# Output projection to gate and up: the decode rows of h stored from another queue, the first pair's gate and up alternating per operand, memory and pools rearranged

## The chip, the core and the metric

The kernel runs on one core of a Trainium2 chip. The metric is device time in microseconds (us), the median over runs of the whole kernel. The core's engines are TensorE (PE in the rows; its weight loads are PEld), VectorE (DVE), ScalarE (ACT), GpSimd (POOL) and SyncE (SP). Each works through its own instructions in a fixed order. Transfers (DMA) are started by an engine and then run by themselves; those that SyncE starts are one queue (SPq), those that GpSimd starts another (POOLq).

## The reference

One step of a hybrid decoder, for 2048 prompt tokens and 8 decode tokens, width 1024 and feed-forward width 2816:

```python
n = rmsnorm(x)
u = n @ w_in                       # one projection, split among A and B
A = sliding-window softmax attention (window 128, sinks, relative bias)
B = gated linear attention (chunked recurrence)
h = x + concat(A, B) @ w_o
z = rmsnorm(h)
y = h + (silu(z @ w_gate) * (z @ w_up)) @ w_down
```

The outputs are y for prompt and decode tokens, and the new key, value and state caches. All of it is float32.

## The kernel before, in words

**Numbers.** A float32 product is made of three matmuls in a faster type. Each operand is split in a high and a low part: ScalarE casts (L92), VectorE subtracts (L93); `mm3` issues high by high, high by low, low by high (L104 to L106).

**Stages.** Projection and attention come first, then gated linear attention, whose results `mix_d` lie in memory off the core. Then come the three stages near the change.

*Output projection* (the block that begins at L963). The tokens are 16 tiles of 128, taken in the order 0, 4, 1, 5, 2, 6, 3, 7, 8, 12 and so on to 11, 15, and then the eight decode rows (tile `NB`). `load_tile` loads a tile of `mix_d` (L995), splits it to `mt` and loads x into `h` (L1000). `product` (L1009) multiplies with the output weights `WO0` and `WO1`, adds into `h` and stores h for the last stage (L1022; for the decode rows to `hdec_d`). `normalise` (L1025) squares on ScalarE, takes the reciprocal root, scales to `z` (L1032), transposes by TensorE (`ps_zT`, L1037) and copies into the blocks `b0` to `b3`. `operands` (L1045) makes seven operands from the four blocks of a tile pair, splits each into a buffer `zhl` and stores it from GpSimd into `zc_d` (L1057). `zhl` comes from a pool of three buffers, so that the fourth operand is cast when the first one's store has landed. The decode rows' four columns per block are appended to the operands of the last tile pair, (1, 3) in the code.

*Gate and up* (the block that begins at L1166). The product z times the weights is done in a Strassen form: seven products P1, P6, P2, P7, P5, P4, P3 in this order (`PRODS`), each on one operand of z (`z0` to `z6`, numbered in that order) and one sum of weight blocks. Each product has its accumulator in one of three kinds of banks in PSUM: a (P1, then P2 on top of it), b (P6, P7, P4), c (P5, then P3). `ready` says what follows each: behind P1, ScalarE copies the bank to `p1` (L1149) before P2 adds into the bank; behind the others come adds on VectorE, and products of gate and up at the end. The 22 column blocks of the weights are 11 pairs (`fp`); the tokens are two halves (`sb`), the first of 512 columns in one piece, the second of 516 in two. For each half, seven loads bring `z0` to `z6` (L1242) from SyncE. For each pair, `load_w` loads four raw pieces of weights (L1179, two of gate and two of up), and `units` and `sums_a` form the sums on VectorE (`sx`, `sy`, L958 and L961) and split them to `whl`. There are four raw buffers and seven `whl` buffers.

*Down* (from L1270) loads `md_d`, forms the Strassen sums of the down weights, and adds h from memory by accumulating transfers; the decode rows go to `hdec_d` in the same manner.

**What sets the order.** The code gives the dependencies and a first order. The framework's scheduler, with a simulation of the engines, then sets the order on each engine; the program waits by semaphores. The pools lie on the right and left side of the on-core memory; where a pool of a later stage lies on the bytes of an earlier one, its first user waits for the earlier users.

**The numbers of the tiles** (as in `z4_10179`) are running numbers of the program and differ between the two kernels.

Of the kernel before, what the change touches and what calls it, by code (L numbers as in the profile page):

```python
# [51 lines left out]
def hymba_kernel(ctx: ExitStack, tc: tile.TileContext, I, O, X=None, phases=3):  # L52
# [49 lines left out]
    def mm3(ps, lh, ll, rh, rl, start, stop, more=False):  # L102

        nc.tensor.matmul(ps, lh, rh, start=start, stop=False, skip_group_check=more)  # L104
        nc.tensor.matmul(ps, lh, rl, start=False, stop=False, skip_group_check=more)  # L105
        nc.tensor.matmul(ps, ll, rh, start=False, stop=stop, skip_group_check=more)  # L106

# [856 lines left out]
    with ExitStack() as ph:  # L964


        mixp = pool(ph, "m_mix", 2, side="right")
        wop = pool(ph, "m_wo", 1, side="right")
        hlp = pool(ph, "m_hl", 3, side="right")
        hp = pool(ph, "m_h", 3, side="right")  # L970
        zp = pool(ph, "m_z", 2, side="right")
        bp = pool(ph, "m_b", 1, side="right")
        tp = pool(ph, "m_t", 1, side="right")
# [3 lines left out]

        WO = [wop.tile([P, 2, KD, 512], F32R, name=f"WO{dh}") for dh in range(2)]
        gBf = zp.tile([P, D], F32, name="gBf", bufs=1)
# [4 lines left out]
        def load_tile(ti):  # L984
            h = hp.tile([P, D], F32, tag="h", name="h")
            if ti == NB:
                nc.sync.dma_start(h[:ND], I["x_sample"].rearrange("n o d -> (n o) d"))
                return None, h

            if ti in tiles[:2]:  # L990
                mr = hlp.tile([P, 1056], F32, tag="hl", name="mr")[:, :1024]
            else:
                mr = craw.tile([P, 1024], F32, tag="raw", name="mr")
            mr = mr.rearrange("p (k t) -> p k t", k=KD)
            nc.sync.dma_start(mr, mix_d[ti])  # L995

            mt = mixp.tile([P, 2 * KD * P + 64], F32R, tag="mix", name="mt")[:, :2 * KD * P]
            mt = mt.rearrange("p (s k t) -> p s k t", s=2, k=KD)
            split(mt[:, 0], mt[:, 1], mr)
            nc.sync.dma_start(h, I["x_prompt"][0, ti * P:(ti + 1) * P, :])  # L1000
            return mt, h
# [8 lines left out]
        def product(ti, mt, h):  # L1010
            n = P if ti < NB else ND
            for dh in range(2):
# [8 lines left out]
                add_h(h, n, dh, ps)  # L1021
            nc.sync.dma_start(h_d[ti] if ti < NB else hdec_d, h[:n])  # L1022
            return h
# [142 lines left out]
    with ExitStack() as ph:  # L1166
        zcp = pool(ph, "g_zc", 1, side="right")

# [14 lines left out]

        def pair(sb, fp, zc):
            W, pieces = WIDTHS[sb], PIECES[sb]
# [17 lines left out]
            def prod(st, q, hl):  # L1203
                z = zc[q]
                hv = hl.rearrange("p s (k n) -> p s k n", k=4)
                for i, (c0, c1) in enumerate(pieces):
                    ps = st.bank(q, i)[:, :c1 - c0]
                    for k in range(4):
                        mm3(ps, hv[:, 0, k], hv[:, 1, k], z[:, 0, k, c0:c1], z[:, 1, k, c0:c1],
                            q in ("P1", "P6", "P5") and k == 0, k == 3, q not in ("P1", "P6", "P5"))  # L1210
# [27 lines left out]
        for sb in range(2):  # L1238
            zc = {name: zcp.tile([P, 2, 4, 516], F32R, tag=f"z{q}", name=f"z{q}")[:, :, :, :WIDTHS[sb]]
                  for q, name in reversed(list(enumerate(PRODS)))}  # L1240
            for q, name in enumerate(PRODS):
                nc.sync.dma_start(zc[name].bitcast(F32), zc_d[sb][q])  # L1242
            for fp in range(NP):
                pair(sb, fp, zc)

# [152 lines left out]
```

## Time and profile before

| what | value |
|---|---|
| three runs | 2311.71, 2314.23, 2313.62 us; median 2313.62 |
| the profiled execution: time, span | 2311.51 us, 2309.7 us |
| transferred in all | 364.57 MB, mean 158 GB/s |
| SyncE's queue (with the other hardware queues) | 258.80 MB, 34.2% of 16 DMA engines |
| GpSimd's queue | 103.55 MB, 17.9% |

The span is the time from the first to the last recorded instruction; 1.8 us of the execution lie outside it. In this span the output projection's last prompt tile ends at 938 us, pair 0 of gate and up begins at 959, and the down stage's first loads come about 1850. In rows of waits, the three numbers behind the colon are the sum of the idle time in us, the number of waits and the longest. In rows of the timeline stand the start in us, the duration, the engine, the line, the operation, out<-in with shapes, the count, and in brackets the idle time ahead with what ended it. A row that begins with A:B is a stretch in us.

### The profile page before, as it was taken

The numbers are of one execution on the slowest core, as the hardware profiler recorded it, in microseconds if no ns is written. First come the engines' busy times: TensorE is split into PE (matmuls) and PEld (weight loads), VectorE is DVE, ScalarE is ACT, GpSimd is POOL, SyncE is SP. The second block draws the span as 40 slices with busy tenths as digits, with TensorE's granted clock in tenths as the row PEclk, the third lists the DMA queues.
The fourth block names the chain that finished last, engine by engine and source line by source line (L and its number), as shares of the span: only waits on it lengthen the run. The fifth ranks groups of instructions, "written<-read, shape, count | busy, mean of one in ns | idle before, by whom it ended". The sixth has DMA issues, their size and how long they took to land.

```text
span 2309.7 us, 34809 instructions
## 1 busy us (share of the span) xinstructions
PE 2227.1 (96%) x12649; PEld 1923.6 (83%) x12649; DVE 1600.5 (69%) x3236; ACT 957.2 (41%) x2120; POOL 623.8 (27%) x791
## 2 busy tenths in 40 slices
PE   8999998999999999699999999999999989999998
PEld 6888886788887788578888889999999968787887
DVE  6787887587776567556666666767676674847477
ACT  5676777343443234323232333333333243535342
POOL 2443434365465133201111110101010122222222
PEclk9999998999998999899999999999999999999999
DMA  7323234245325689872324257323233277878877
GB/s 239 122 75 115 93 108 153 90 157 165 126 87 214 225 275 288 276 247 87 119 79 127 78 177 290 110 84 115 87 111 97 83 225 171 210 165 213 185 184 263
DMA packets 204935, 364.57 MB, mean 158 GB/s; under 512 B 15411, under 2 KB 128332, under 8 KB 200780
## 3 DMA queue, kind: packets, MB, share of 16 engines
q1 hardware_dynamic: 167740, 258.80, 34.2%
q0 software_dynamic: 37024, 103.55, 17.9%
q8 instruction: 100, 1.64, 0.3%
q14 instruction: 71, 0.58, 0.1%
HBM read 211.09 MB, written 152.27 MB: 157 GB/s over the span
## 4 chain that ended last, share of the span: by engine, by line
PE 31%; issue 20%; POOL 5%; DMA 1%; DVE 0%; POOLq 0%; ACT 0%; SPq 0%; DVEq 0%; ACTq 0%
PE ps_b L105 4%; PE ps_b L104 4%; PE ps_b L106 4%; POOL h_d L1329 4%; PE ps_c L105 3%; PE ps_c L104 3%; PE ps_c L106 3%; PE ps_a L105 3%; PE ps_a L106 3%; PE ps_a L104 3%; POOL out_y_prompt_dram L1324 1%; DMA z<-zc_d_P 1%; POOL md_d L1236 1%; DMA zc_d_P<-zhl 0%; DMA wrg<-in_w_gate_dram 0%
## 5 line engine op out<-in xcount | busy, mean ns | idle before, releaser
L104 PE MATMUL ps_b<-z,whl 128*128 128x258 f32 (+1 forms) x792 | 253.8, 321 | 3.2 <-DMA z<-zc_d_P 3.2
L105 PE MATMUL ps_b<-z,whl 128*128 128x258 f32 (+1 forms) x792 | 254.0, 321 | 0.0
L106 PE MATMUL ps_b<-z,whl 128*128 128x258 f32 (+1 forms) x792 | 252.8, 319 | 0.0
L92 ACT CAST dm<-mr 128x384 fp32r<-128x384 f32 (+1 forms) x224 | 108.0, 488 | 188.4 <-PE ps_b L106 97.6
L104 PE MATMUL ps_a<-z,whl 128*128 128x258 f32 (+1 forms) x528 | 170.9, 324 | 8.3 <-DMA z<-zc_d_P 8.3
L105 PE MATMUL ps_a<-z,whl 128*128 128x258 f32 (+1 forms) x528 | 170.7, 323 | 0.0
L106 PE MATMUL ps_a<-z,whl 128*128 128x258 f32 (+1 forms) x528 | 170.3, 323 | 0.0
L104 PE MATMUL ps_c<-z,whl 128*128 128x258 f32 (+1 forms) x528 | 168.6, 319 | 0.9 <-DMA z<-zc_d_P 0.9
L105 PE MATMUL ps_c<-z,whl 128*128 128x258 f32 (+1 forms) x528 | 169.1, 320 | 0.0
L106 PE MATMUL ps_c<-z,whl 128*128 128x258 f32 (+1 forms) x528 | 168.9, 320 | 0.0
L104 PEld LDWEIGHTS ps_b<-z,whl 128*128 128x128 f32 x792 | 149.3, 189 | 15.9 <-DMA z<-zc_d_P 3.5
L106 PEld LDWEIGHTS ps_b<-z,whl 128*128 128x128 f32 x792 | 149.2, 188 | 12.1
L105 PEld LDWEIGHTS ps_b<-z,whl 128*128 128x128 f32 x792 | 149.2, 188 | 11.9
L93 DVE TENSOR_TENSOR dm<-mr,dm 128x384 fp32r<-128x384 f32 (+1 forms) x224 | 114.9, 519 | 59.4 <-ACT dm L92 59.4
L92 ACT CAST whl<-wrg 128x512 fp32r<-128x512 f32 x132 | 81.6, 620 | 150.5 <-PE ps_b L106 81.2
L802 POOL TENSOR_TENSOR bd<-E,qTb 64x128 f32<-64x128 f32 x224 | 127.1, 567 | 60.6 <-ACT E L787 47.2
L93 DVE TENSOR_TENSOR whl<-wrg,whl 128x512 fp32r<-128x512 f32 x132 | 90.9, 688 | 42.9 <-ACT whl L92 42.7
L961 DVE TENSOR_TENSOR gu<-ps_c,gu 128x512 f32<-128x512 f32 (+1 forms) x130 | 77.9, 600 | 61.0 <-PE ps_c L106 60.3
L1236 POOL DMA_DIRECT2D md_d<-m x22 | 15.7, 713 | 373.7 <-DVE m L1199 360.3
L104 PEld LDWEIGHTS ps_a<-z,whl 128*128 128x128 f32 x528 | 100.8, 191 | 17.0 <-issue 4.4
L104 PEld LDWEIGHTS ps_c<-z,whl 128*128 128x128 f32 x528 | 99.8, 189 | 9.3 <-ACT whl L92 1.3
L105 PEld LDWEIGHTS ps_a<-z,whl 128*128 128x128 f32 x528 | 100.5, 190 | 8.2
(385 smaller groups left out, 6625.9 us busy)
## 6 DMA issues: line engine op xcount, KB each, us to landing
mr<-md_d SPq DMA_DIRECT2D x24, 1344.0 KB
zc_d_P<-zhl POOLq DMA_DIRECT2D x49, 512.0 KB, 6.1
wrg<-in_w_gate_dram SPq DMA_DIRECT2D x44, 512.0 KB
wrg<-in_w_up_dram SPq DMA_DIRECT2D x44, 512.0 KB
nT_d<-nT SPq DMA_DIRECT2D x16, 1024.0 KB
zT<-nT_d SPq DMA_DIRECT2D x8, 2048.0 KB
z<-zc_d_P SPq DMA_DIRECT2D x7, 2064.0 KB
z<-zc_d_P SPq DMA_DIRECT2D x7, 2048.0 KB
```

Of the source, the lines that this page charges most:

```text
L92: nc.scalar.copy(h, src)
L93: (eng or nc.vector).tensor_tensor(l, src, h.bitcast(F32), ALU.subtract)
L104: nc.tensor.matmul(ps, lh, rh, start=start, stop=False, skip_group_check=more)
L105: nc.tensor.matmul(ps, lh, rl, start=False, stop=False, skip_group_check=more)
L106: nc.tensor.matmul(ps, ll, rh, start=False, stop=stop, skip_group_check=more)
L802: nc.gpsimd.tensor_tensor(bv[rows, :, h], eo, qo, ALU.mult)
L961: nc.vector.tensor_tensor(out, a, b, ALU.add)
L1236: nc.gpsimd.dma_start(md_d[sb][g][:, :, q, fp - GROUPS[g][0], :], src.rearrange("p (m t) -> p m t", m=4))
L1324: nc.gpsimd.dma_start(O["y_prompt"][0, ti * P:(ti + 1) * P, cols], hq[which])
L1329: nc.gpsimd.dma_start(h_d[ti][:, cols], c, accum_op=ALU.add)
```

## The change

It has five parts.

1. The decode rows' h is stored to `hdec_d` from GpSimd and no longer from SyncE.
2. The pool of `WO0` and `WO1` becomes two pools, the pool of `zhl` lies behind that of `z`, and the mix tile is padded by 96 in place of 64 elements (17152 bytes a partition in place of 16896).
3. `z0` to `z6` get a pool each, allocated from P1 on; before, they were one pool and allocated from the back. By the program's memory map, `z0` to `z2` (P1, P6, P2) now lie on the mix tiles and `WO0`, `z3` and `z4` (P7, P5) on `WO1`, `z5` and `z6` on `h`, `z` and `zhl`. Before, `z0` lay at the far end and `z4` on `zhl` buffers.
4. The raw weights of a half's first pair are loaded ahead of the loads of z in the code, and those of each further pair behind the code of the pair before it.
5. For the first half's first pair, each of the 14 products is put behind the one before it in the order (`issue_after`), so that gate and up alternate per operand.

```diff
-            nc.sync.dma_start(h_d[ti] if ti < NB else hdec_d, h[:n])
+            (nc.sync if ti < NB else nc.gpsimd).dma_start(h_d[ti] if ti < NB else hdec_d, h[:n])
```
```diff
         mixp = pool(ph, "m_mix", 2, side="right")
-        wop = pool(ph, "m_wo", 1, side="right")
-        hlp = pool(ph, "m_hl", 3, side="right")
+        wop = [pool(ph, f"m_wo{dh}", 1, side="right") for dh in range(2)]
         hp = pool(ph, "m_h", 3, side="right")
         zp = pool(ph, "m_z", 2, side="right")
+        hlp = pool(ph, "m_hl", 3, side="right")
...
-            mt = mixp.tile([P, 2 * KD * P + 64], F32R, tag="mix", name="mt")[:, :2 * KD * P]
+            mt = mixp.tile([P, 2 * KD * P + 96], F32R, tag="mix", name="mt")[:, :2 * KD * P]
```
```diff
-        zcp = pool(ph, "g_zc", 1, side="right")
+        zcp = {name: pool(ph, f"g_z{q}", 1, side="right") for q, name in enumerate(PRODS)}
...
-            ug, uu = load_w(w_g, fp), load_w(w_u, fp)
             if len(pieces) == 1:
+                last = None
                 for q in PRODS:
-                    prod(sg, q, next(ug))
-                    prod(su, q, next(uu))
+                    for st, us in ((sg, ug), (su, uu)):
+
+                        with tc.issue_after(last) if fp == 0 and last else nullcontext():
+                            last = prod(st, q, next(us))
...
         for sb in range(2):
-            zc = {name: zcp.tile([P, 2, 4, 516], F32R, tag=f"z{q}", name=f"z{q}")[:, :, :, :WIDTHS[sb]]
-                  for q, name in reversed(list(enumerate(PRODS)))}
+            zc = {name: zcp[name].tile([P, 2, 4, 516], F32R, tag=f"z{q}", name=f"z{q}")[:, :, :, :WIDTHS[sb]]
+                  for q, name in enumerate(PRODS)}
+            raws = load_w(w_g, 0), load_w(w_u, 0)
             for q, name in enumerate(PRODS):
                 nc.sync.dma_start(zc[name].bitcast(F32), zc_d[sb][q])
             for fp in range(NP):
-                pair(sb, fp, zc)
+                pair(sb, fp, zc, *raws)
+                if fp + 1 < NP:
+                    raws = load_w(w_g, fp + 1), load_w(w_u, fp + 1)
```

`mm3` returns its last matmul, and `prod` the instruction of it. From L1022 on, a line of the kernel before has a number 1 to 6 higher in the changed one (L1022 is L1023, L1057 is L1058, L1149 is L1150, L1179 is L1181, L1242 is L1248).

**SyncE, at the end of the output projection.** What stands in its order before, from the last prompt tile's store of h on (`wrg` is a raw piece of weights, the last row the first piece of pair 1):

```order
L1022 DMA h_d15_4838<-h_9846 128x1024
L1022 DMA hdec_d_4839<-h_9962 8x1024
L1242 DMA z0_10184<-zc_d0_P1_4840 128x8x512
L1242 DMA z1_10183<-zc_d0_P6_4841 128x8x512
L1242 DMA z2_10182<-zc_d0_P2_4842 128x8x512
L1242 DMA z3_10181<-zc_d0_P7_4843 128x8x512
L1242 DMA z4_10180<-zc_d0_P5_4844 128x8x512
L1242 DMA z5_10179<-zc_d0_P4_4845 128x8x512
L1242 DMA z6_10178<-zc_d0_P3_4846 128x8x512
L1179 DMA wrg_10475<-in_w_gate_dram 128x4x256
```

And in the changed kernel, at the same place (`wrg_10490` is pair 1's second gate piece, `wrg_10492` and `wrg_10494` its two up pieces):

```order
L1248 DMA z0_10200<-zc_d0_P1_4840 128x8x512
L1023 DMA h_d15_4838<-h_9849 128x1024
L1248 DMA z1_10201<-zc_d0_P6_4841 128x8x512
L1248 DMA z2_10202<-zc_d0_P2_4842 128x8x512
L1248 DMA z3_10203<-zc_d0_P7_4843 128x8x512
L1248 DMA z4_10204<-zc_d0_P5_4844 128x8x512
L1181 DMA wrg_10490<-in_w_gate_dram 128x4x256
L1181 DMA wrg_10492<-in_w_up_dram 128x4x256
L1248 DMA z5_10205<-zc_d0_P4_4845 128x8x512
L1248 DMA z6_10206<-zc_d0_P3_4846 128x8x512
L1181 DMA wrg_10494<-in_w_up_dram 128x4x256
```

The store of `hdec_d` is gone from this queue, P1's load stands ahead of the last prompt tile's store, and two of pair 1's pieces stand between the loads of P5 and P4.

**VectorE, at the operands of the last token tile.** Before (`zhl` rows are the second half of a split of these operands, `sx` is a sum of raw pieces, `gu2` the add on P6's bank of the gate):

```order
L93 TENSOR_TENSOR zhl_10134<-b1_9843,zhl_10134 128x528
L93 TENSOR_TENSOR zhl_10138<-t2_10120,zhl_10138 128x528
L93 TENSOR_TENSOR zhl_10142<-t0_10118,zhl_10142 128x528
L93 TENSOR_TENSOR zhl_10146<-t3_10121,zhl_10146 128x528
L93 TENSOR_TENSOR zhl_10150<-b3_9845,zhl_10150 128x528
L93 TENSOR_TENSOR whl_10331<-sx_10262,whl_10331 128x512
L961 TENSOR_TENSOR sx_10262<-wrg_10203,wrg_10205 128x512
L93 TENSOR_TENSOR whl_10348<-sx_10241,whl_10348 128x512
L961 TENSOR_TENSOR gu2_10194<-ps_b_10248,gp1_10193 128x512
```

And in the changed kernel (`zhl_10137` to `zhl_10153` are the same five operands; `uu2` is the add on P6's bank of up):

```order
L93 TENSOR_TENSOR whl_10407<-wrg_10209,whl_10407 128x512
L93 TENSOR_TENSOR zhl_10137<-b1_9846,zhl_10137 128x528
L958 TENSOR_TENSOR sy_10538<-wrg_10490,sx_10537 128x512
L93 TENSOR_TENSOR zhl_10141<-t2_10123,zhl_10141 128x528
L93 TENSOR_TENSOR zhl_10145<-t0_10121,zhl_10145 128x528
L958 TENSOR_TENSOR sx_10558<-wrg_10492 128x512
L93 TENSOR_TENSOR zhl_10149<-t3_10124,zhl_10149 128x528
L93 TENSOR_TENSOR zhl_10153<-b3_9848,zhl_10153 128x528
L961 TENSOR_TENSOR gu2_10224<-ps_b_10270,gp1_10223 128x512
L961 TENSOR_TENSOR uu2_10227<-ps_b_10291,up1_10226 128x512
```

Two sums of pair 1, which read `wrg_10490` and `wrg_10492`, have moved between the splits of the operands.

On ScalarE, before and now, the casts of the last tile's operands stand ahead of the copies of P1's banks. On TensorE, P1's products of gate and up (24 matmuls) now stand ahead of the transposes of the decode rows, and pair 1's first product no longer stands between products of pair 0.

More of the change, by code (lines that the diff above doesn't have):

```diff
@@ L1 @@
 import math
-from contextlib import ExitStack
+from contextlib import ExitStack, nullcontext
 import numpy as np
@@ L105, in mm3 @@
         nc.tensor.matmul(ps, lh, rl, start=False, stop=False, skip_group_check=more)
-        nc.tensor.matmul(ps, ll, rh, start=False, stop=stop, skip_group_check=more)
+        return nc.tensor.matmul(ps, ll, rh, start=False, stop=stop, skip_group_check=more)
     def rstd(ss, n, scale, cols=1):
@@ L975, in hymba_kernel @@
         acc = pool(ph, "m_acc", 4, space=PSUM)
-        WO = [wop.tile([P, 2, KD, 512], F32R, name=f"WO{dh}") for dh in range(2)]
+        WO = [wop[dh].tile([P, 2, KD, 512], F32R, name=f"WO{dh}") for dh in range(2)]
         gBf = zp.tile([P, D], F32, name="gBf", bufs=1)
@@ L1182, in load_w, with pair @@
             return units((r0[:, :, 0:P], r1[:, :, 0:P], r0[:, :, P:], r1[:, :, P:]), sums_a)
-        def pair(sb, fp, zc):
+        def pair(sb, fp, zc, ug, uu):
             W, pieces = WIDTHS[sb], PIECES[sb]
```

5 lines of the change are left out of this document (3 added, 2 removed).

## The prediction, made before the changed kernel was run

> **What bounds the kernel now.** The page comes first: how full TensorE is.
>
> ```profile
> span 2309.7 us, 34809 instructions
> PE 2227.1 (96%) x12649; PEld 1923.6 (83%) x12649; DVE 1600.5 (69%) x3236; ACT 957.2 (41%) x2120; POOL 623.8 (27%) x791
> z<-zc_d_P SPq DMA_DIRECT2D x7, 2048.0 KB
> wrg<-in_w_gate_dram SPq DMA_DIRECT2D x44, 512.0 KB
> ```
>
> TensorE is the bound; time is only won where it stands still or runs at a lowered clock. The last two rows, from the page's DMA issues, give sizes: an operand load of the first token half has 2048 KB, a raw weight piece 512 KB. Next I read TensorE's waits from 935 to 1000 us, where the change acts.
>
> ```profile
> PE ps_a L104 <- DMA z<-zc_d_P: 8.3, 2, 4.3
> PE ps_zT L1037 <- DVE z L1032: 6.9, 1, 6.9
> PE ps_b L104 <- DMA z<-zc_d_P: 3.2, 2, 3.0
> PE ps_c L104 <- DMA z<-zc_d_P: 0.9, 1, 0.9
> ```
>
> So 12.4 us go to the operand loads and 6.9 us to the normalisation of the decode rows. The stage table (PE, PEld, DVE, ACT, POOL busy, granted clock, DMA share, GB/s) shows a lowered clock too, then a saturated DMA, then a full TensorE:
>
> ```profile
> 960.00:965.00 5.00, 5.00 (x13) 3.84 (x13) 0.00 (x0) 0.32 (x1) 0.71 (x1) 0.51 1.03 373
> 995.00:1000.00 5.00, 4.07 (x18) 3.03 (x17) 1.99 (x3) 0.62 (x1) 0.00 (x0) 1.00 1.04 397
> 1000.00:1020.00 20.00, 20.00 (x88) 16.18 (x87) 11.72 (x20) 6.92 (x12) 1.42 (x2) 1.00 0.58 198
> ```
>
> TensorE's timeline dates each landing by the matmul that waited for it: the last prompt tile's last matmul, then the first matmuls of P1, P6, P2, P7, P5, then pair 1's first and one after pair 0's last product.
>
> ```profile
> 937.38 0.39 PE L106 MATMUL ps_wo<-WO,mt 128*128 128x512 f32 x1
> 959.10 0.80 PE L104 MATMUL ps_a<-z,whl 128*128 128x512 f32 x1 [4.28 <-DMA z<-zc_d_P]
> 964.81 0.46 PE L105 MATMUL ps_a<-z,whl 128*128 128x512 f32 x1
> 970.62 0.51 PE L104 MATMUL ps_b<-z,whl 128*128 128x512 f32 x1 [3.02 <-DMA z<-zc_d_P]
> 982.03 0.76 PE L104 MATMUL ps_a<-z,whl 128*128 128x512 f32 x1 [4.03 <-DMA z<-zc_d_P]
> 989.61 0.47 PE L104 MATMUL ps_b<-z,whl 128*128 128x512 f32 x1 [0.23 <-DMA z<-zc_d_P]
> 996.34 0.47 PE L104 MATMUL ps_c<-z,whl 128*128 128x512 f32 x1 [0.93 <-DMA z<-zc_d_P]
> 1001.98 0.40 PE L104 MATMUL ps_a<-z,whl 128*128 128x512 f32 x1
> 1015.92 0.40 PE L104 MATMUL ps_a<-z,whl 128*128 128x512 f32 x1
> ```
>
> P5's 24 matmuls take 1001.98 - 996.34 = 5.64 us, 0.235 us each. From 996.34 on nothing waits. At 1015.92 pair 0 is done and 12 matmuls of pair 1 besides (2.8 us), so the mark for equal work is 1013.1: "pair 0 done, nothing more". The forecast is the difference of that mark.
>
> The reason for the late loads is SyncE's queue:
>
> ```profile
> SPq L1022 <- DVE h L582: 11.4, 1, 11.4
> ```
> ```profile
> 950.34 0.29 SPq L1022 DMA_DIRECT2D hdec_d<-h  x1
> 950.81 15.16 SPq L1242 DMA_DIRECT2D z<-zc_d_P  x4
> 991.56 5.48 SPq L1179 DMA_DIRECT2D wrg<-in_w_gate_dram  x1
> ```
>
> The decode rows' store waits 11.4 us for its add, with the seven loads behind it.
>
> **What the change takes away.** The store leaves that queue, and P1's load now waits only for the mix tiles: 937.38 + 0.39, so it is issued at 937.8 instead of 950.81, 13.0 us earlier. The store's place on GpSimd is before the decode rows' reciprocal root; its data is ready at 950.3, the root's about 1.2 us later, and an issue takes 0.85 us: nothing. TensorE's order puts P1 ahead of the decode transposes, which covers the 6.9 us. P6 and P2 need WO0 free, P7 and P5 WO1, each free by 946; P5's load no longer waits for operand stores. Taken alone these edits win what the loads come earlier.
>
> **What it adds.** The rows of order show two pieces of pair 1's raw weights between P5's and P4's loads, and on VectorE two sums of pair 1 that read them, between the operand stores of the last token tile. Both are new places. Does a piece behind P5's load land behind it? Before, the first such piece was issued at 991.56, behind all seven loads; this is its sum on VectorE:
>
> ```profile
> 1009.75 0.69 DVE L958 TENSOR_TENSOR sy<-wrg,sx 128x512 f32<-128x512 f32 x1 [1.29 <-DMA wrg<-in_w_gate_dram]
> ```
>
> It took 18.2 us, 13.4 us after P5's load: the queue delivers in turn. That gives prices: two loads and one piece (a quarter of a load) in 13.41 us are 5.96 us a load and 1.5 us a piece. Beside stores it is dearer:
>
> ```profile
> 938.03 0.85 POOL L1057 DMA_DIRECT2D zc_d_P<-zhl  x1 [0.34 <-DVE zhl L93]
> ...
> 947.30 0.85 POOL L1057 DMA_DIRECT2D zc_d_P<-zhl  x1 [1.46 <-DVE zhl L93]
> ...
> 976.67 0.85 POOL L1057 DMA_DIRECT2D zc_d_P<-zhl  x1 [3.53 <-DVE zhl L93]
> ```
> ```profile
> zc_d_P<-zhl POOLq DMA_DIRECT2D x7, 528.0 KB, 9.4
> ```
> ```profile
> DMA to landing us min/median/max: 4.2/7.5/10.8
> ```
>
> Seven stores fall beside P6's and P2's loads, which took 982.03 - 959.10 = 22.93 us: (22.93 - 11.92) / 7 = 1.57 us a store. P1's own 8.29 us are a load, a store and 0.7 us to start.
>
> Now the new wait, step by step.
> 1. P5's load lands: 937.8 + 0.7 + five loads 29.8 + the last h store 1.5 + seven stores 11.0 (four issued from 938.03 to 947.30, three of the last tile before the sum) = 980.8. The piece behind it: 982.3. It has been issued in time: it needs P6's up product, which ends near 966 (P1's load 950.8, P1 with a cold clock, P6).
> 2. VectorE stands at the sum until then. Behind it wait four operand splits of the last tile, then the adds on P6's bank. Sum and next split 2 x 0.69 = 1.4: 983.7.
> 3. The split's store takes 7.5 us to land: 991.2. There are three hl buffers, so the fourth of these operands is cast only when this store has landed.
> 4. ScalarE casts in that order and copies P1's bank behind the casts. Before, it was so too:
>
> ```profile
> 963.96 0.63 PE L106 MATMUL ps_a<-z,whl 128*128 128x512 f32 x1
> ```
> ```profile
> 974.71 0.63 ACT L92 CAST zhl<-b 128x528 fp32r<-128x528 f32 x1 [3.45 <-DMA zc_d_P<-zhl]
> 975.25 0.58 ACT L1149 COPY gp<-ps_a 128x512 f32<-128x512 f32 x1
> ```
>
> P1's gate product ended at 964.6, and its copy ran at 975.25, right behind the last cast; then it cost nothing, since P2's load came at 982.03. P2 adds into the same bank and must wait for the copy. Cast and copy 1.2: P2 starts at 992.4.
> 5. Five products of 24 matmuls: 28.2. TensorE has stood still for some 26 us and is cold: after the wait at 959.10 thirteen matmuls took 5.71 us to 964.81 instead of 3.06, so 2.6. Pair 0 ends at 1023.2, **10.1 us behind** the mark of 1013.1.
>
> On step 5, the Trainium skill, "TensorE: Matmul & The Clock Gate", "Part 1: The HAM clock gate", says that an idle window of about 3.4 us halves the clock and 3.4 us of work restore it. By that the cold start would lose 1.7 instead of 2.6 us and the sum would be 9.2, an estimate from the page; the row here shows a longer cold stretch, 5.7 us.
>
> Bounds. The loads with stores, h and piece are 15.25 MB; at the table's best 397 GB/s 38.4 us, so the piece at 976.9; a store landing in 4.2; 1.5 us for the cold start (seven slow matmuls after 982.03): +0.3 us in all. Upwards: three loads at 11.5 us as seen beside stores, then 7.6 and 6.7, the h store, the piece and 0.7: 990.2; a store in 10.8: +21.3 us. I take the middle prices, measured on the same kinds of transfer.
>
> What is late next: P4's bank also waits for a sum that reads the third piece, behind P3's load, behind the last operand store. That store 1000.0, load 1006.7, piece 1008.2, sum and add 1009.6; P4 is due at 992.4 + 2.6 + 16.9 = 1011.9. Cover 2.3 us; with a store of 10.8 us it is gone and costs 1.0.
>
> Elsewhere. At the projection's start WO1 is loaded first and tile 4's split comes earlier, which covers 1.1 us, but tile 1's mix load now stands behind tile 4's h store:
>
> ```profile
> 757.15 0.50 PE L106 MATMUL ps_wo<-WO,mt 128*128 128x512 f32 x1 [1.14 <-DVE mt L93]
> 771.82 0.50 PE L104 MATMUL ps_wo<-WO,mt 128*128 128x512 f32 x1 [3.02 <-ACT mt L92]
> ```
> ```profile
> 765.69 2.50 SPq L995 DMA_DIRECT2D mr<-mix_d  x3
> 768.68 0.32 SPq L1022 DMA_DIRECT2D h_d<-h  x1
> ```
>
> That can be 3.0 us later and lengthen the 3.02 us wait. Between -1.1 and +3.0 I take 0, since both are near. In down the decode matmuls move a few places within a stretch that stands still for its loads:
>
> ```profile
> 1850.00:1860.00 10.00, 6.48 (x16) 3.97 (x17) 10.00 (x20) 6.63 (x14) 2.32 (x4) 0.54 1.01 396
> ```
>
> I take 0, with -1 to +1. The second half's loads, the padding and the split pools in themselves cost nothing: TensorE waits for no operand load there.
>
> **The sum.** The profiled execution's own time, 2311.5 us (span 2309.7), plus 10.1 is 2321.6. The three runs' median is 2313.6, 2.1 above it; on it the forecast is 2323.7.
>
> **Rivals.**
> *The loads win* (12 in 100, faster). If the piece overtakes P5's load, because it is small or the sixteen DMA engines don't keep step, VectorE never holds ScalarE. It decides at P2's start: earlier than 982.7 wins. Then P5 starts at 980.8, P4's load (two pieces ahead) lands at 989.8, P3's at 995.8, pair 0 ends at 1001.4: 11.7 us won, 2301.9. For it speak 13 us of earlier issue; against it the piece at 1009.75, which did not overtake. The Trainium skill, "DMA: Bandwidth & Descriptors", "Two DMAs through the same engine are not ordered", says that nothing orders DMAs across the 16 engines; the trace shows no overtaking.
> *It cancels out* (16). Fast stores (4.2 us) and loads at 397 GB/s bring P2 to 984 to 987: between +0.3 and +4.6, about 2316.
> *A second wait* (8). The thin cover goes and the early stage takes its 3.0 us besides: 10.1 + 1.0 + 3.0 or more, about 2328 and beyond.
> *The forecast* has 64.
>
> **How the numbers follow.** 0.2% is 4.6 us, about what a measurement of this kernel tells from no change. Slower by more: 64 and 8 of the cases, 0.72. Within: 0.16. Faster: 0.12. The range leaves out the faster case and the far end of the bounds: 2313 to 2332.
>
> **What would show it.** A wait of TensorE at P2's first matmul of 20 us or more, put down to ScalarE's copy of P1's bank; on VectorE an idle time ended by a raw gate piece, in the middle of the last tile's splits, near 982; P1's first matmul near 951. No wait for the decode transposes. Wrong: P2 starting on its load, or the sum on VectorE finding its piece before 975.

## The result, and the profile after

The changed kernel took 2328.71 us (median of 4 runs, 2327.68 to 2331.72) against 2313.93 for the kernel before on the same chip. The ratio is 1.0073, 95% interval 1.0060 to 1.0086: **14.8 us slower**. The forecast was 10.1 us slower (2323.7, range 2313 to 2332). The profiled executions differ by more, 2329.41 - 2311.51 = 17.9 us, because before's profiled run lies 2.4 us below the median of its four runs and after's 0.7 above. One execution in the whole set, in experiment 11, took 5114.89 us and is in no ratio.

The page of the changed kernel: the same matmuls and bytes in a longer span.

```profile
span 2327.6 us, 34823 instructions
PE 2228.0 (96%) x12649; PEld 1926.0 (83%) x12649; DVE 1598.7 (69%) x3236; ACT 957.4 (41%) x2120; POOL 623.0 (27%) x792
```

TensorE's waits from 930 to 1040 us (sum, number, longest) answer to the four rows of before:

```profile
PE ps_a L104 <- ACT gp L1150: 28.0, 1, 28.0
PE ps_a L104 <- DMA z<-zc_d_P: 6.5, 1, 6.5
```

Before, 12.4 us went to operand loads and 6.9 to the decode rows. Now one wait of 28.0 us stands there, and what ends it is ScalarE's copy of P1's bank. TensorE's timeline gives the places: the last prompt matmul, P1's first matmul, the decode transposes, P2's first matmul, the first matmul behind pair 0, the last matmul of the kernel.

```profile
940.94 0.39 PE L106 MATMUL ps_wo<-WO,mt 128*128 128x512 f32 x1
...
957.02 0.77 PE L104 MATMUL ps_a<-z,whl 128*128 128x512 f32 x1 [6.52 <-DMA z<-zc_d_P]
...
965.22 0.66 PE L1038 MATMUL ps_zT<-ident,z 8*128 8x8 f32 x8
999.75 0.80 PE L104 MATMUL ps_a<-z,whl 128*128 128x512 f32 x1 [27.98 <-ACT gp L1150]
...
1029.39 0.40 PE L104 MATMUL ps_a<-z,whl 128*128 128x512 f32 x1
...
2316.30 0.39 PE L106 MATMUL ps_c<-dhl,dm 128*128 128x512 f32 x1
```

Pair 0 ends at 1029.39, 16.3 us behind the mark of 1013.1. The chain that leads to 999.75 is read backwards on ScalarE, GpSimd, VectorE and SyncE. ScalarE's last operand cast and, right behind it, the copy:

```profile
998.58 0.63 ACT L92 CAST zhl<-b 128x528 fp32r<-128x528 f32 x1 [14.39 <-DMA zc_d_P<-zhl]
999.12 0.58 ACT L1150 COPY gp<-ps_a 128x512 f32<-128x512 f32 x1
```

The cast had waited 14.4 us for a store to free a buffer. That store is the first of these three, issued by GpSimd, which had waited 16.5 us for the split:

```profile
991.39 2.68 POOL L1058 DMA_DIRECT2D zc_d_P<-zhl  x3 [16.48 <-DVE zhl L93]
```

The split stood on VectorE behind the sum of pair 1, and the sum behind its raw piece:

```profile
973.07 0.70 DVE L93 TENSOR_TENSOR zhl<-b,zhl 128x528 fp32r<-128x528 f32 x1
989.78 0.69 DVE L958 TENSOR_TENSOR sy<-wrg,sx 128x512 f32<-128x512 f32 x1 [16.01 <-DMA wrg<-in_w_gate_dram]
990.39 1.32 DVE L93 TENSOR_TENSOR zhl<-t,zhl 128x528 fp32r<-128x528 f32 x2
```

VectorE did nothing for 16.0 us, with a ready split behind the waiting sum. SyncE's queue shows why the piece came so late; it stands behind P5's load:

```profile
941.36 0.59 SPq L1248 DMA_DIRECT2D z<-zc_d_P  x1
942.09 0.58 SPq L1023 DMA_DIRECT2D h_d<-h  x1
945.94 21.99 SPq L1248 DMA_DIRECT2D z<-zc_d_P  x4
968.03 10.10 SPq L1181 DMA_DIRECT2D wrg<-in_w_gate_dram  x1
```

P1's load is issued 9.4 us earlier than before (941.36 against 950.81), yet P1 starts only 2.1 us earlier (957.02 against 959.10). The stage table (PE, PEld, DVE, ACT, POOL busy, granted clock, DMA share, GB/s) from 940 to 990, before:

```profile
940.00:990.00 50.00, 31.55 (x117) 22.56 (x115) 21.54 (x37) 15.49 (x26) 9.68 (x12) 0.80 0.97 318
```

and in the changed kernel:

```profile
940.00:990.00 50.00, 25.17 (x110) 17.46 (x108) 18.94 (x33) 11.06 (x19) 8.52 (x11) 0.79 1.02 339
```

The DMA engines were at 0.97 of their time in this stretch already (the share is a sum of the packets' times and can pass 1). They are at 1.02 now; there was hardly a gap for the earlier loads to fill.

**The account.** Every kernel here has 12649 matmuls, so the start of the same-numbered matmul can be compared with before's. The table gives what each stage adds, in us, for the profiled execution of each kernel. The stages are cut at the matmuls that start, in before's profile, at 730 (9 us ahead of the projection's first), at 790 (in the projection's fourth tile), at 920 and at 1021 (so that the block holds pair 0); then come the start of down, 1840 to 1920, and what lies between the last matmul and the end. What a table row leaves over is at most 0.7, but for 2.1 of "pad 64" at the end of down. The names are those of the experiments below.

| kernel | to 730 | to 790 | to 920 | block | down's start | last matmul, in all | behind it |
|---|---|---|---|---|---|---|---|
| after | +1.3 | +0.8 | +1.2 | +12.9 | -2.4 | +13.8 | +4.05 |
| sums held | +1.5 | +1.3 | +1.2 | +2.4 | -1.8 | +4.4 | +4.04 |
| transposes first | -2.2 | -1.3 | +1.2 | +12.2 | -1.9 | +8.0 | +4.04 |
| both | -0.3 | -1.0 | +1.2 | +3.3 | -2.0 | +1.7 | +4.04 |
| before, GpSimd store | +1.5 | -1.4 | 0.0 | +0.6 | -0.1 | +0.6 | +4.05 |
| four buffers | +3.4 | +0.7 | +1.2 | +14.5 | -2.3 | +18.0 | +4.05 |
| pieces last | -1.0 | +0.9 | +1.2 | +12.2 | -2.0 | +11.3 | +4.05 |
| before, ScalarE store | -1.9 | +2.3 | -0.1 | 0.0 | +1.5 | +2.2 | 0.00 |
| before, GpSimd store in halves | -0.4 | -0.9 | 0.0 | +0.7 | +0.9 | +0.2 | +4.05 |
| pad 64 | +3.9 | +0.8 | -0.3 | +11.8 | -2.5 | +15.8 | +4.05 |
| before, pad 96 | -0.3 | +0.2 | +1.4 | -0.8 | 0.0 | +0.8 | +0.01 |
| held, ScalarE store | +2.2 | -0.5 | +1.1 | +4.7 | -2.4 | +5.0 | +0.05 |
| before, rows of 512 | +1.4 | -1.9 | 0.0 | +1.4 | +1.6 | -3.0 | +0.01 |

The stretch to 730 is the same code, in the same order, in all of them and varies from -2.2 to +3.9, so a single profile's total is only good to some us; the stages are compared one by one. (In the last row the stage between the block and down brings another -6.2.) For the changed kernel three terms stand out besides the block: 1.2 us inside the projection, -2.4 in down, and 4.05 us behind the last matmul. That last one is seen in two rows, the last output store and the span's end. Before (whose span ends at 2309.7):

```profile
2304.67 0.54 POOL L1324 DMA_DIRECT2D out_y_prompt_dram<-hq  x1 [0.82 <-DVE hq L961]
```

After (span 2327.6):

```profile
2318.44 0.54 POOL L1332 DMA_DIRECT2D out_y_prompt_dram<-hq  x1 [0.82 <-DVE hq L961]
```

From that store to the end it is 5.1 us before and 9.1 after. In the trace's instruction records the difference is one instruction, GpSimd's closing drain: 4.316 us before, 8.357 after.

### The profile page after: what moved, and what is told of

Read it like the earlier page. It is cut to its first block, busy times and chain, and to the rows that moved or that the text cites. A ratio compares the mean times of both kernels' runs of the same rounds, so it can differ in the third digit from the quotient of the medians.

```text
span 2327.6 us, 34823 instructions
## 1 busy us (share of the span) xinstructions
PE 2228.0 (96%) x12649; PEld 1926.0 (83%) x12649; DVE 1598.7 (69%) x3236; ACT 957.4 (41%) x2120; POOL 623.0 (27%) x792
## 4 chain that ended last, share of the span: by engine, by line
PE 58%; issue 22%; POOL 8%; DVE 5%; DMA 4%; ACT 2%; SPq 0%; POOLq 0%; ACTq 0%; DVEq 0%
PE ps_b L105 5%; PE ps_b L104 4%; PE ps_b L106 4%; POOL h_d L1337 3%; PE ps_a L105 3%; PE ps_c L105 3%; PE ps_a L104 3%; PE ps_a L106 3%; PE ps_c L106 3%; PE ps_c L104 3%; PE ps_d L104 3%; PE ps_d L106 3%; PE ps_d L105 3%; PE ps_wo L104 2%; PE ps_wo L105 2%
## 5 line engine op out<-in xcount | busy, mean ns | idle before, releaser
L105 PEld LDWEIGHTS ps_b<-z,whl 128*128 128x128 f32 x792 | 148.8, 188 | 11.8
L92 ACT CAST whl<-sy 128x512 fp32r<-128x512 f32 x88 | 54.6, 620 | 130.4 <-PE ps_b L106 86.8
```

The source lines that it names most:

```text
L92: nc.scalar.copy(h, src)
```

## The experiments

**1 to 3: is it the sum of pair 1?** In the first, pair 1's sums are put on VectorE behind the add on P7's bank of up in pair 0 (`add` returns its instruction for this); the loads stay as they are.

```diff
-                add(u3, ps, p1)
+                self.mark = add(u3, ps, p1)
...
-                            last = prod(st, q, next(us))
+                            with tc.issue_after(marks[0]) if (sb, fp) == (0, 1) else nullcontext():
+                                hl = next(us)
+                            last = prod(st, q, hl)
+                marks.append(su.mark)
```

> The changed kernel, with pair 1's first sums on VectorE put behind the P7 adds of pair 0; nothing else is edited. Theory A (the sum that waits for its piece holds the operand splits, these the store, the buffer, ScalarE and P2): VectorE's wait of 16 us for the raw piece goes; the second half-operand's store goes out near 978, lands near 987, P2 starts near 988 in place of 999.75, and the time falls by about 11.5 us from 2328.7 to 2317 (2314 to 2320). Rival B (the loads set the pace, DMA engines are full from 947 to 990, and the sum only stands in the same time): at most 3 us, 2326. Rival C (TensorE's order is the cause: P1 ahead of the decode transposes makes the operands late): no gain from this edit, 2327 to 2329.

Measured: 2319.44 against 2315.59 before on that chip, 1.0019 (1.0010 to 1.0028): some 4 us of the 14.8 are left. TensorE's waits in the block:

```profile
PE ps_a L104 <- ACT gp L1150: 16.1, 1, 16.1
```

P2 starts at 989.64 instead of 999.75, and the block costs 2.4 us instead of 12.9. The sum in the middle of the splits was the cause of 10.5 us. What holds P2 now is the same copy, behind a last cast at 988.47 that waits 3.4 us for a store. Before, that cast ran at 974.71.

In the second, P1 goes behind the decode transposes, as before the change; the scheduler then puts the sum two splits later. `zt` collects the transposes; its last is the decode rows'.

```diff
-                last = None
+                last = zt[-1]
```

> The changed kernel, with TensorE's P1 of pair 0 put behind the transposes of the decode rows, as it was before. The scheduler then also sets the sum two splits later on VectorE: the fourth and fifth operand of the last tile are split ahead of it. Theory A: operands begin 5 to 6 us earlier, ScalarE is no longer held and P2 starts near 983, but the adds on P6's bank still stand behind the sum, which waits for its piece until 990: the wait moves to P7, near 993, and the time is 2316 (2313 to 2319). Rival B (loads): 2326 or more. Rival C (the transposes alone): the whole loss and more comes back, 2309 to 2312, with no wait of VectorE for the piece that anyone waits for.

Measured: 2326.56, 1.0054 (1.0040 to 1.0067); a miss by 10 us. P2 came at 984.03, 10 us earlier than in the changed kernel once the 5.6 us are taken off by which this execution came earlier into the block; and the block still cost 12.2. VectorE's rows for the sums, in this kernel:

```profile
990.25 0.69 DVE L958 TENSOR_TENSOR sy<-wrg,sx 128x512 f32<-128x512 f32 x1 [17.12 <-DMA wrg<-in_w_gate_dram]
...
1008.92 0.69 DVE L958 TENSOR_TENSOR sy<-wrg,sx 128x512 f32<-128x512 f32 x1 [12.89 <-DMA wrg<-in_w_up_dram]
```

and TensorE's for P7 and P4:

```profile
993.69 0.50 PE L104 MATMUL ps_b<-z,whl 128*128 128x512 f32 x1 [2.29 <-DVE gu L961]
...
1010.27 0.50 PE L104 MATMUL ps_b<-z,whl 128*128 128x512 f32 x1 [3.63 <-DVE gu L961]
```

The sum no longer holds the splits, but it still holds VectorE until 990; the add on P6's bank stands behind it, and P7 needs that bank. The third piece does the same to P4 at 1008.92. The wait moved from one bank to the next. The third kernel holds the sums and puts the transposes first as well.

> Both edits together: sums of pair 1 behind the P7 adds, P1 behind the decode transposes. Theory A: P2 near 982, P7 near 988, P5 on its load near 990 to 993, pair 0 done some 18 us earlier than in the changed kernel: 2310 (2307 to 2313), below the sum of neither edit alone, since both serve the same chain. Rival B (loads): 2326. Rival C: as with the transposes alone, within 1 us of that run.

Measured: 2319.59, 1.0020 (1.0010 to 1.0029), the same as with the sums held alone, where 2310 was expected. P2 starts at 986.88, with this wait:

```profile
PE ps_a L104 <- ACT gp L1152: 12.3, 1, 12.3
```

The decode transposes being late is not what keeps the held kernel from winning: moving them up left the last cast at 985.71, 11 us later than before (974.71). The stores that these casts wait for are not slower than before: those of 528 KB take 8.8 us to land here and 9.4 before (medians). But the first of the seven casts comes 6.2 us later (960.86 against 954.69), behind 512 KB stores that take 9.7 us to land instead of 4.6, and ScalarE's rows show something more behind the second:

```profile
963.09 0.63 ACT L92 CAST zhl<-t 128x528 fp32r<-128x528 f32 x1 [1.59 <-DVE t L958]
966.24 0.62 ACT L92 CAST whl<-sx 128x512 fp32r<-128x512 f32 x1 [2.52 <-PE ps_a L106]
969.02 0.62 ACT L92 CAST whl<-sx 128x512 fp32r<-128x512 f32 x1 [2.16 <-PE ps_a L106]
971.81 0.62 ACT L92 CAST whl<-sx 128x512 fp32r<-128x512 f32 x1 [2.17 <-PE ps_b L106]
972.34 0.63 ACT L92 CAST zhl<-b 128x528 fp32r<-128x528 f32 x1
```

Three casts of weight sums, each waiting for TensorE, stand between the second and the third operand. Before, the third was cast at 957.45, right behind the second at 956.91. From the first cast to the last it is 24.9 us here and 20.0 before. The changed kernel has weight casts among the operand casts too, at 969.86 and 971.81. No run moves them away, so what they cost is not shown.

**4, 7 and 8: what are the earlier loads worth?** The kernel before, with the `hdec_d` store alone moved to GpSimd:

```diff
-            nc.sync.dma_start(h_d[ti] if ti < NB else hdec_d, h[:n])
+            (nc.sync if ti < NB else nc.gpsimd).dma_start(h_d[ti] if ti < NB else hdec_d, h[:n])
```

> The kernel before, with the one edit that the decode rows' h is stored from GpSimd. Order and memory are else those of before: the seven loads stand together, no sum of pair 1 among the splits. Theory A: P1's load goes out some 12 us earlier, P1 starts near 955, P2 on ScalarE's copy or its load near 976 to 979, P5's load still waits for the last operand's store, P5 near 991: 4 to 6 us won, 2309 (2306 to 2312). Rival B (the DMA engines are the limit): under 2 us won, 2312 to 2314. Rival D (GpSimd's queue is held by the new store and the operand stores go out later): slower than before, 2315 or more.

Measured: 2319.45, 1.0019 (1.0009 to 1.0029): slower by some 4 us, where a gain was expected; a miss. SyncE issued the loads 11.2 us earlier:

```profile
939.61 52.83 SPq L1242 DMA_DIRECT2D z<-zc_d_P  x7
```

But TensorE's timeline for P1, P6, P2 and P7 reads almost as before (959.10, 970.62, 982.03, 989.61):

```profile
959.48 0.80 PE L104 MATMUL ps_a<-z,whl 128*128 128x512 f32 x1 [2.84 <-DMA z<-zc_d_P]
969.18 0.67 PE L104 MATMUL ps_b<-z,whl 128*128 128x512 f32 x1 [2.49 <-DMA z<-zc_d_P]
979.83 0.77 PE L104 MATMUL ps_a<-z,whl 128*128 128x512 f32 x1 [3.28 <-DMA z<-zc_d_P]
990.00 0.77 PE L104 MATMUL ps_b<-z,whl 128*128 128x512 f32 x1 [2.93 <-DMA z<-zc_d_P]
```

The stage table says why:

```profile
940.00:990.00 50.00, 30.05 (x115) 21.23 (x114) 22.53 (x38) 15.59 (x26) 10.96 (x14) 0.83 1.03 327
```

The DMA engines go from 0.97 to 1.03 busy and move 327 instead of 318 GB/s: over 50 us that is 0.45 MB, about a fifth of one load. What the loads take early, the stores lose: the three 512 KB stores of `zc_d` after 940 take 10.8 us to land instead of 4.6 (medians). So the block gains nothing (+0.6). The slowdown lies at the other end of the kernel; its last output store is at 2305.24 and its span ends at 2314.4, 9.1 us later, with the drain of 8.357 us.

The same store from ScalarE's queue instead (`nc.scalar` in place of `nc.gpsimd`):

> The kernel before, with the decode rows' h stored from ScalarE's queue in place of SyncE's: the loads are freed as with the store on GpSimd, and GpSimd gets no further transfer. Theory E (found in the profiles: GpSimd's last instruction, a drain, takes 4.3 us in the kernel before and 8.4 us in every kernel with the store on GpSimd): drain 4.3 us, the time 3 to 4 us under that of the kernel before with the store on GpSimd, so the same as the kernel before within 2 us (2312 to 2316). If the drain's length is chance or a matter of timing: as with the store on GpSimd, 4 us above the kernel before. The block of pair 0 itself as there: within 1 us of before, since the DMA engines are full from 940 on.

Measured: 2314.68, 1.0001 (0.9991 to 1.0010). The last output store, in this kernel, whose span ends at 2311.9:

```profile
2306.84 0.54 POOL L1324 DMA_DIRECT2D out_y_prompt_dram<-hq  x1 [0.82 <-DVE hq L961]
```

That is 5.1 us, and the drain is 4.316 again. The loads were issued at 939.58, as early as in the other, and the block cost 0.0. So the longer drain comes with the store on GpSimd's queue, and the earlier issue is worth nothing by itself. P2 started at 978.76 here, after a wait of 6.2 us for the copy of P1's bank: even in before's order the copy is the next thing behind the loads. P7 at 989.55 was again the load's.

Is the price paid per transfer? The store from GpSimd in two halves:

```diff
-            nc.sync.dma_start(h_d[ti] if ti < NB else hdec_d, h[:n])
+            if ti < NB:
+                nc.sync.dma_start(h_d[ti], h[:n])
+            else:
+                for dh in range(2):
+                    nc.gpsimd.dma_start(hdec_d[:, dh * 512:(dh + 1) * 512], h[:n, dh * 512:(dh + 1) * 512])
```

> The kernel before, with the decode rows' h stored from GpSimd in two halves, two transfers in place of one. Theory E with a price for each transfer: the drain takes 12 us. With a fixed price for the 8-row store or its place: 8.4 us. If it hangs on whether the count is even or odd: 4.3 us again. The rest as with one store.

Measured (a single run): 2315.79, drain 8.357 again. The price is not one per transfer of this store. GpSimd starts 346 transfers before, 347 with this store and 348 with its halves; whether any other further transfer would do the same was not tried.

**5 and 6: two other ways around the sum.** A fourth buffer for the splits, at the price of one of the three `h` buffers:

```diff
-        hp = pool(ph, "m_h", 3, side="right")
+        hp = pool(ph, "m_h", 2, side="right")
...
-        hlp = pool(ph, "m_hl", 3, side="right")
+        hlp = pool(ph, "m_hl", 4, side="right")
```

> The changed kernel with four buffers for the split operands in place of three, paid for by two buffers for h in place of three. The sum of pair 1 stays where it is on VectorE. Theory A, its buffer step: the last cast on ScalarE now needs the third operand's store and no longer the fourth's, which stands behind the sum; so ScalarE copies P1's bank near 985 and P2 starts near 985 in place of 999.75, while VectorE still waits for the piece until 990, and the adds on P6's bank make P7 wait until 993 or 994: 10 to 13 us of the block come back, 2316 to 2319, plus 0 to 4 us if two h buffers hold the projection up. Rival B (the loads): P2 and P7 move by under 3 us. If the buffer step is wrong, and ScalarE or P2 hangs on VectorE directly: P2 stays at 999.

Measured: 2333.51 against 2314.66, 1.0080 (1.0064 to 1.0096); a miss, slower than the changed kernel. TensorE's waits:

```profile
PE ps_b L104 <- DVE gu L961: 11.3, 2, 7.4
PE ps_a L104 <- ACT gp L1150: 11.1, 1, 11.1
```

P2 came at 987.72, 12 us earlier than in the changed kernel, though this execution came 2.0 us later into the block; so the buffer step of the chain is real. The block cost 14.5 all the same: the sums, at 996.00 and 1018.73, now held P7 and P4 by VectorE's adds.

Pair 1's pieces put behind all seven loads on SyncE, as before the change:

```diff
-                nc.sync.dma_start(zc[name].bitcast(F32), zc_d[sb][q])
+                zl = nc.sync.dma_start(zc[name].bitcast(F32), zc_d[sb][q]).ins
...
-                    raws = load_w(w_g, fp + 1), load_w(w_u, fp + 1)
+                    with tc.issue_after(zl) if (sb, fp) == (0, 0) else nullcontext():
+                        raws = load_w(w_g, fp + 1), load_w(w_u, fp + 1)
```

> The changed kernel, with the raw pieces of pair 1 put behind the seven loads of z in SyncE's order; nothing is edited on VectorE, but the scheduler, which sees the pieces later, now sets the sums behind all splits by itself. Theory A: the wait of VectorE for a piece is gone as in the run with the sums held, and P1's load, no longer behind the first piece, comes about 1 us earlier: P2 near 987, 2316 to 2319. Rival B: 2326.

Measured: 2327.05, 1.0054 (1.0040 to 1.0067); a miss. The sums left the splits, but stood ahead of the adds on P7's banks in pair 0 while their pieces came later still. VectorE, and TensorE's wait for P4's product behind it:

```profile
1009.38 0.69 DVE L958 TENSOR_TENSOR sx<-wrg 128x512 f32<-128x512 f32 x1 [11.81 <-DMA wrg<-in_w_gate_dram]
```
```profile
1013.66 0.51 PE L104 MATMUL ps_b<-z,whl 128*128 128x512 f32 x1 [4.02 <-DVE gu L961]
```

P2 waited 18.2 us, until 991.19. Moving the piece on SyncE alone does not help; the sum has to leave its place ahead of pair 0's adds on VectorE too, as in the first experiment.

**9 and 10: the padding.** In the changed kernel, the 617 matmuls of the projection between 790 and 920 take 1.2 us longer. Its timeline shows two stretches of 42 matmuls each, in neighbouring tiles:

```profile
859.34 0.39 PE L104 MATMUL ps_wo<-WO,mt 128*128 128x512 f32 x1
...
869.10 0.39 PE L104 MATMUL ps_wo<-WO,mt 128*128 128x512 f32 x1
...
871.36 0.39 PE L104 MATMUL ps_wo<-WO,mt 128*128 128x512 f32 x1
...
880.88 0.39 PE L104 MATMUL ps_wo<-WO,mt 128*128 128x512 f32 x1
```

9.76 us and 9.52 us: 232 and 227 ns a matmul. The tiles alternate so throughout; before, all take 227 to 228. The two mix buffers lie 17152 / 2 = 8576 bytes apart now, 8448 before; by the memory map their addresses modulo 256 are 224 and 96 now, and both 224 before. In these matmuls the mix tile is the operand of 128 columns that is loaded as weights; `WO`, with 512 columns, is the one streamed against it, and it lies at the same place for every tile. The changed kernel with 64 elements of padding, and the kernel before with 96:

```diff
-            mt = mixp.tile([P, 2 * KD * P + 96], F32R, tag="mix", name="mt")[:, :2 * KD * P]
+            mt = mixp.tile([P, 2 * KD * P + 64], F32R, tag="mix", name="mt")[:, :2 * KD * P]
```

The second makes the same edit the other way round.

> The changed kernel with the mix tile padded by 64 elements again; the order on every engine is that of the changed kernel. It asks about the projection's matmuls, which follow one another every 227.1 to 233.3 ns (third and second matmul of three, and the first) in every kernel with the old memory and every 229.6 to 235.0 ns in every kernel with the new, 1.2 us over 617 matmuls. If the padding does it: 227 ns again, 1.2 us less in this stretch, about 2327. If the place of the pools does it: 229.6 ns, 2329. If it is a matter of the transfers beside them: something between, with no fixed number.

> The kernel before with the mix tile padded by 96 elements, its other pools as they were. If the padding alone makes the projection's matmuls slower: 229.6 ns, 1.2 us more over 617 matmuls, 2315. If it needs the new order of the pools: 227.1 ns, 2313.6.

Measured (a single run each): the 617 matmuls take -0.3 us against before with 64 in the changed kernel, +1.4 with 96 in the kernel before, where the tiles alternate at 228 and 232 ns too. The totals, 2331.41 and 2312.41, are single runs and carry the chance of the early stages (+3.9 and -0.3). The padding is worth 1.2 to 1.4 us to the matmuls that read the tile.

**11: are these two causes the whole loss?** Sums held (experiment 1) and the `hdec_d` store from ScalarE.

> The changed kernel with both causes taken away that the runs point to: the sums of pair 1 behind the P7 adds, and the decode rows' h stored from ScalarE's queue in place of GpSimd's. Theory A and E together: the 9 to 11 us of the block and the 4.0 us of GpSimd's last drain come back, so the time is that of the kernel before within its uncertainty: 2313 to 2316, GpSimd's drain 4.3 us, P2 near 988. If a third cause of some microseconds is left: 2317 or more. If the early issue of the loads is worth something after all: 2311 or less.

Measured: 2316.27 against 2314.71, 1.0004 (0.9994 to 1.0014): no difference from before. The sum's place and the drain account for the loss to within what is measured. What else the change wins (2.4 in down) and loses (the padding, the rest of the block) about cancels.

**12: addresses as a lever.** If an operand's address moves the matmuls' spacing, gate and up, with about 5500 of the 12649 matmuls, should show it. Here the edit moves the streamed operand, `z`, and not the one loaded as weights. In the kernel before, the rows of `z` are laid out with 512 instead of 516 elements for the first half, and three of the buffers are made larger by 96:

```diff
-            zc = {name: zcp.tile([P, 2, 4, 516], F32R, tag=f"z{q}", name=f"z{q}")[:, :, :, :WIDTHS[sb]]
-                  for q, name in reversed(list(enumerate(PRODS)))}
+            zc = {name: zcp.tile([P, 4224 if q < 3 else 4128], F32R, tag=f"z{q}", name=f"z{q}")[:, :8 * WIDTHS[sb]].rearrange(
+                "p (s k t) -> p s k t", s=2, k=4) for q, name in reversed(list(enumerate(PRODS)))}
```

> The kernel before, with the operands z of the first half laid out in rows of 512 elements in place of 516, and three of the seven buffers enlarged by 384 bytes, so that P1, P6, P2 and P3 begin at an address that leaves 480 when divided by 512, P7 at 352, P5 at 224, P4 at 96; each operand's load becomes one run of 16384 bytes a partition in place of eight of 2048. It tries the placing that the padding pointed to on the 1848 matmuls of the first half, which follow one another every 232.3 ns, where the projection's and the down stage's come every 227. If the address of the streamed operand is what counts (WO at 480: 227.1; WO at 224: 229.6): 227 in P1, P6, P2, P3, 229.6 in P5, in all 3 to 5 ns a matmul or 6 to 10 us less, 2304 to 2308. If the row length doesn't matter: 232.3 again, and the time within 2 us of the kernel before. The loads: with longer runs either as before, since the bytes count, or faster by up to 5 us.

Measured: 2310.14 against 2314.57, **0.9975 (0.9965 to 0.9985)**: faster than both kernels. The stage from 1100 to 1300, where TensorE never waits, before and then in this kernel:

```profile
1100.00:1300.00 200.00, 200.00 (x862) 161.75 (x861) 132.73 (x205) 61.29 (x102) 25.20 (x35) 1.00 0.34 103
```
```profile
1100.00:1300.00 200.00, 200.00 (x877) 164.22 (x876) 132.62 (x206) 62.48 (x105) 25.20 (x35) 1.00 0.34 105
```

15 more matmuls fit in 200 us at the same clock. Worked out from the starts of its matmuls, the spacing is 227 ns in the products whose operand lies at 224 modulo 256 (P1, P6, P2, P5, P3) and 233 in the two at 96 (P7, P4). Before, it is 232 to 233 in all; there the rows of 516 elements start 16 bytes further modulo 256 from one to the next. Within this kernel all rows have 512 elements, so the address alone parts P7 and P4 from the others; that the row length has no share in the gain against before is not shown. That is 6.2 us over the first half. The loads move in packets of 16384 instead of 2048 bytes here, and that gave the block nothing: P2 waited 10.1 us, until 984.02, for the copy of P1's bank.

## Why the prediction was right, and where its sizes were off

*The chain* was right at every step: sum held by its piece behind P5's load, split, store, buffer, cast, copy, P2. The wait at P2's first matmul (20 us or more forecast, 28.0 measured), the releaser (the copy) and the idle time on VectorE in the middle of the splits stood where the text had put them (the idle time ended at 989.8 instead of 982), and the waits for the decode rows and for P7's and P5's loads are gone. Experiment 1 shows the sum to be the cause: 10.5 of the block's 12.9 us go with it.

*The piece's landing* was mis-sized: 982.3 forecast, 989.8 measured, 7.5 late. The projection ended 3.6 us later than in before's profile (1.3 before 730, 0.8 on to 790, 1.2 by the padding, and 0.3 besides), so P1's load was issued at 941.36 and not at 937.8. The other 3.9 lie in the transfers: from this issue to the piece's sum it took 48.4 us, where the forecast had 44.5 to the landing. They began with P1's own load: "P1's first matmul near 951" was 957.02, 15.7 us from the issue instead of 13.0.

*Store and buffer* were right: 7.2 us from the split's store at 991.39 to the cast at 998.58, against 7.5.

*The cold start* was priced at 2.6 us from P1's row. TensorE's timeline of the changed kernel behind 999.75, where the seventh, ninth and tenth matmul of P2 are:

```profile
1002.48 0.63 PE L104 MATMUL ps_a<-z,whl 128*128 128x512 f32 x1
1003.33 0.44 PE L106 MATMUL ps_a<-z,whl 128*128 128x512 f32 x1
1003.61 0.39 PE L104 MATMUL ps_a<-z,whl 128*128 128x512 f32 x1
```

The first nine matmuls took 3.86 us from 999.75 to 1003.61, against 2.09 at 0.232 each: 1.8. At P1, in the same trace, the slow stretch lasted 5.3 us, from 957.02 to 962.28. The Trainium skill ("TensorE: Matmul & The Clock Gate", "Part 1: The HAM clock gate") has half speed for about 3.4 us of work, which gives 1.7, an estimate from the page. At P2 the trace is close to that; at P1 its slow stretch is longer.

*"Taken alone these edits win what the loads come earlier"* was wrong. Experiments 4 and 7 issue them 11 us earlier and the block gains 0. The forecast knew the saturated DMA (a share of 1.03 and more) but priced the earlier loads one by one, as if the queue alone had held them back. By the rows of 940 to 990 the share could rise only from 0.97 to 1.03, and the bytes by 3%. By these runs its rival "the loads win", at 2301.9, was out of reach.

*The store on GpSimd, "nothing"*, was wrong by 4.05 us. It costs nothing where it stands, as was said; the price is paid at the kernel's end, in GpSimd's closing drain. No row of before could show it.

*"The padding ... cost nothing"* was wrong by 1.2 us (experiments 9 and 10).

*"TensorE's order puts P1 ahead of the decode transposes, which covers the 6.9 us"* was half right: that wait is gone, but the transposes come at 965.22 instead of 953.83, and the operand casts with them. Experiment 3 shows that it makes no difference to the time, since ScalarE's casts hold P2 then.

*What is late next*: the thin cover at P4 broke in experiments 2, 5 and 6, as named; in 2 and 5 P7 came with it, which was not.

*Down* was taken as 0, with -1 to +1. It is -2.4, and -1.8 to -2.5 in all eight kernels with the changed order, -0.1 to +1.6 in the five without. *The early stage* was taken as 0 between -1.1 and +3.0, and is +0.8; kernels with the order of before lie there between -1.9 and +2.3, so no effect of the change is shown.

The sum, then: the block's mark 16.3 late, of which 12.9 arose in the block, 2.0 in the projection and 1.3 by chance before it; -2.4 in down; 4.05 at the end. That is 17.9, and 14.8 between the medians. A block mis-sized by 2.8 and a drain that was not foreseen moved the result 5 us from the forecast. That it stayed inside the range is in part luck: down gave 2.4 back, and the range had not been drawn for a price at the kernel's end.

**Open.** Why the drain is 4.04 us longer for one store of eight rows, when GpSimd issues many other transfers in both kernels, was not settled. Nor why the address matters to a matmul, nor where the 2.4 us in down come from. Four split buffers with all three of `h` were not tried; nor was the layout of experiment 12 in the changed kernel, nor the weight casts moved from between the operand casts on ScalarE.

## What to carry to other kernels

An instruction that waits for a late transfer holds all that stands behind it on its engine (here VectorE for 16.0 us): look at what stands behind it, and follow the chain to the matmul that starts last. Loads issued 11 us earlier won nothing here, on DMA engines at 0.97 of their time; read that share before counting the microseconds of earlier issue. When an edit moves a transfer to another queue, compare the end of the kernel too.

## What the runs showed of the hardware

- One 32 KB store of eight rows from GpSimd's queue made its closing drain 8.357 instead of 4.316 us, whether in one transfer or two, in every kernel that had it; from SyncE it was 4.316, from ScalarE 4.316 and, in experiment 11, 4.357.
- At a granted clock of 1.00, 512-column matmuls were spaced 227 ns with an operand at 224 modulo 256 bytes and 232 to 233 ns with it at 96, by the memory map. In the projection this was the operand loaded as weights (the mix tile); in gate and up of experiment 12, with rows of 512 elements, it was the streamed one (`z`).
- Loads and stores on different queues share the DMA engines' time: with the loads issued 11.2 us earlier (experiment 4), the three 512 KB stores after 940 landed in 10.8 instead of 4.6 us (medians), and the DMA share went from 0.97 to 1.03.
